# A gated three-branch decoder layer: order of the paired projections, start plan, queue of the merge stores and spacing of the convolution inputs

## The chip, the cores and the metric

The kernel runs on one core of a Trainium2 chip. A core has five engines that run side by side, each through its own list of instructions in order: TensorE (PE, matmuls; the profile shows its weight loads apart as PEld), VectorE (DVE), ScalarE (ACT), GpSimd (POOL) and SyncE (SP, which here only issues DMA transfers). They wait for each other through semaphores. Matmuls read SBUF, the core's working memory, and write PSUM, eight banks of 128 x 512 numbers in float32; DVE and ACT take results out of PSUM. The metric is the time of one execution on the device, in microseconds (us).

## The reference

One layer on x of 1024 positions by 1024 channels (D), everything in float32. Cut to what matters:

```python
u = layer_norm(x) * (1 + scale) + shift            # shift, scale, gate from silu(c) @ w_ada
proj = u @ w_in + b_in                             # 1024 x 12288
a_v, a_g, b_b, b_c, b_h, b_g, c_a, c_b, c_g, merge = split(proj)
y_a = (pool(a_v) grouped @ pool_w) * pool_scale * silu(a_g)      # windows 2, 4, 8, 16
y_b = b_b * dwconv3(b_c * b_h) * silu(b_g)
h_c = dwconv31(c_a * sigmoid(c_b))
y_c = silu(layer_norm(h_c)) * silu(c_g)
m = sum_k sigmoid(merge_k) * (y_k @ w_branch[k])
out = layer_norm(ALPHA * x + gate * (m @ w_out))
```

## The kernel before

**Number form.** Every float32 operand of a matmul is split into a high part (written by ACT, rounded to the fast matmul type) and a low part (DVE: the operand minus its high part). One product of two operands is three matmuls, low x high, high x low and high x high, into one PSUM bank (`mm3`, line 132 is the matmul).

**Channels lie on the partitions**, 128 at a time; one tile is 128 channels by 1024 positions, in two halves of 512. u is transposed at the start, scaled and shifted per channel, and split.

**The work is a list of jobs.** A `Job` is one block of 128 output channels: 16 blocks of input, 48 matmuls. Only the first four jobs (c_a and c_b of two channel blocks) and those of the merges are of this kind. All other projections are 46 `Pair`s: two blocks of 128 output columns at once, as a 2 x 2 block product with seven half-size products in place of eight (84 matmuls of 512 columns). For that, sums and differences of the blocks of u (T1 to T4, made once) and of the weights (S1 to S4, for each pair) are formed on DVE. The seven products, in the order of the program, with their banks and weight tiles:

| product | bank | weights | then |
|---|---|---|---|
| A11 x B11 | px | wa | ACT copies px to the left half of r1 (line 520) |
| A12 x B21 | py | wa | DVE adds py to it (523) |
| S1 x T1 | pz | wb | ACT copies pz to r2 (525) |
| S2 x T2 | px, on top | wb | ACT copies px to the right half of r1 (529) |
| S3 x T3 | px, on top | wc | DVE adds px to r2 (531) |
| S4 x B22 | pz, on top | wc | DVE adds pz to r1 (533) |
| A22 x T4 | px, on top | wd | the pair's `after` takes px as the left half of r2 |

wa, wb and wc of a pair take the three buffers of one pool in turn; so the wb of the next pair takes the buffer of this pair's wb, once S2 has read it. wd has one buffer. Six PSUM banks are there for two pairs.

**What sets the order.** The program issues everything in one order, and the Tile framework's scheduler then moves instructions on each engine by a timeline model of its own. Up to the first pair it doesn't: there the table `START` lists every step by hand, in the order in which it is issued (`p031` is one partial product of job 0, input tile 3, half 1; `T2a`, `T2h0`, `T2l0` the sums for T of channel pair 2, `wah`, `S12` steps of the first pair's weights, and so on). A dependence that only orders, and waits for nothing, is put in by `after(late, early)` with the help of `marks`.

**The convolution of 31 taps** runs on DVE, one instruction of 128 x 1024 for each tap (line 605), eight channel blocks, 240 taps. `conv_step` issues six taps after each job, if an input is there. The inputs come from pairs named c2 to c7, put into the list of jobs at every sixth place. A finished block is stored to DRAM and added to a sum over all channels for the LayerNorm; the first block is copied to a tile of its own for that, `hsum` (615).

**The merges.** After the pairs come 24 jobs z (y_k times w_branch[k], 48 matmuls each, gated by DVE), with the four small pool jobs between the first four. Their inputs (y, the pooled values, the gates, the conv's results) were stored to DRAM by earlier stages and are loaded again by POOL's queue (lines 653, 729, 763, 800, 801, 822); stores go by POOL too (538), and weights by SP's queue (381). A queue issues strictly in order: an entry that waits holds all behind it. Nearly all large tiles share one pool of 37 slots of 128 x 1024.

Of the kernel before, what the change touches and what calls it, by code (L numbers as in the profile page):

```python
# [9 lines left out]
F32 = mybir.dt.float32  # L10
# [6 lines left out]
P = 128  # L17
# [10 lines left out]


ADA_PE = (2, 0, 0, 0)  # L30
LN_ACT = (4, 5, 6, 7)
LOADS = "x0 x1 x2 x3 a0 w0 x4 x5 x6 x7 w1 a2 w2 a4 a6 w3"
START = (
# [12 lines left out]
)  # L46

BIG_SLOTS = 37
# [10 lines left out]
def kernel(  # L59
# [23 lines left out]
    wspl = ctx.enter_context(tc.tile_pool(name="wspl", bufs=W8_BUFS))  # L83
    wsum = ctx.enter_context(tc.tile_pool(name="wsum", bufs=2))
    wlast = ctx.enter_context(tc.tile_pool(name="wlast", bufs=1))
    small = ctx.enter_context(tc.tile_pool(name="small", bufs=4))
    ps_main = ctx.enter_context(tc.tile_pool(name="ps_main", bufs=6, space=PSUM))
    ps_misc = ctx.enter_context(tc.tile_pool(name="ps_misc", bufs=2, space=PSUM))
# [41 lines left out]
    def mm3(ps, wh, wl, rh, rl, start, stop):  # L130
        for n, (w, r) in enumerate(((wl, rh), (wh, rl), (wh, rh))):
            nc.tensor.matmul(  # L132
                ps, w, r, start=start and n == 0, stop=stop and n == 2, skip_group_check=True
            )


    ident = const.tile([P, P], F32, name="ident")
    make_identity(nc, ident)
# [15 lines left out]
    def columns(name, parts, q, cols=None):  # L154

        n = sum(a.shape[0] for a in parts)
        rows = slot(f"{name}_rows")[:n, :P]
        at = 0
        for a in parts:
            q.dma_start(out=rows[at : at + a.shape[0], :], in_=a)  # L160
            at += a.shape[0]
        if cols is None:
            cols = const.tile([P, n], F32, name=name)
        ps = misc_ps(f"{name}_ps")
        nc.tensor.transpose(ps[:, :n], rows, ident[:n, :n])
        nc.scalar.copy(cols, ps[:, :n])
        return cols
# [278 lines left out]
    class Pair:  # L446
# [26 lines left out]
        def step(self, what):  # L473

            raw1, raw2 = self.raw
            a1, a2 = (r.rearrange("p (i q c) -> p q i c", q=2, c=P) for r in self.raw)
            if what[0] == "S":
                t = wsum.tile([P, 2, HALF], F32, tag="sum", name=f"s{what[1:]}_{self.name}")
                self.sums[what[1]] = t.rearrange("p n c -> p (n c)")
                one, two = (t[:, n].rearrange("p (i c) -> p i c", c=P) for n in range(2))  # L480
                if what == "S12":
                    nc.vector.tensor_add(one, a2[:, 0], a2[:, 1])
                    nc.vector.tensor_sub(two, one, a1[:, 0])
                    self.s2 = two
                else:
                    nc.vector.tensor_sub(one, a1[:, 0], a2[:, 0])
                    nc.vector.tensor_sub(two, a1[:, 1], self.s2)
                return
            which, high = what[1], what[2] == "h"
            if high and which == "d":  # L490
                self.w[which] = wlast.tile([P, 2, HALF], F32R, tag="last", name=f"wd_{self.name}")
            elif high:
                self.w[which] = wspl.tile([P, 2, D], F32R, tag="w", name=f"w{which}_{self.name}")
            hi, lo = (self.w[which][:, n] for n in range(2))
            if which == "d":
                src = a2[:, 1]
                hi, lo = (t.rearrange("p (i c) -> p i c", c=P) for t in (hi, lo))
            else:
                src = raw1 if which == "a" else self.sums["1" if which == "b" else "3"]
            if high:  # L500
                nc.scalar.activation(hi, src, AF.Identity)
            else:
                marks["split"] = nc.vector.tensor_tensor(
                    out=lo, in0=src, in1=f32(hi), op=ALU.subtract
                )

        def product(self, ps, left, right, first):
            which, block = self.left[left]
            w = self.w[which]
            for i in range(4):  # L510
                ks = slice(block(i) * P, (block(i) + 1) * P)
                rh, rl = quarter(right, i)
                mm3(ps, w[:, 0, ks], w[:, 1, ks], rh, rl, first and i == 0, i == 3)

        def run(self):
            col1, col2 = self.cols
# [77 lines left out]
    def conv_step(n):  # L594
        while n > 0 and conv_todo:
            item = conv_todo[0]
            j, g, h, s = item
            w = cfw_cols[:, (K31 - 1 - s) * NT + j : (K31 - 1 - s) * NT + j + 1]
            if s == 0:
                h = item[2] = slot(f"h{j}")  # L600
                ins = nc.scalar.activation(h, g, AF.Identity, bias=vec("cf_b", j), scale=w)  # L601
                if j == 0:
                    after(ins, marks["u"])
            else:
                nc.vector.scalar_tensor_tensor(  # L605
                    out=h[:, s:], in0=g[:, : S - s], scalar=w, in1=h[:, s:],
                    op0=ALU.mult, op1=ALU.add,
                )
                n -= 1
            item[3] = s + 1  # L610
            if s == K31 - 1:
                conv_todo.popleft()
                if conv["sum"] is None:
                    conv["sum"] = slot("hsum")
                    nc.scalar.copy(conv["sum"], h)
                else:
                    nc.vector.tensor_add(conv["sum"], conv["sum"], h)
                store(h_dram[j], h)
                conv["n"] += 1
# [35 lines left out]
    def a_pool(g):  # L655
        def run(w):
            for o in range(2):
                ct = 2 * g + o
                ps = [bank(f"pool_ps{ct}_{h}") for h in range(2)]
                for i in range(2):  # L660
                    for h in range(2):
                        ph, pl = pooled[2 * g + i]
                        ws = slice((2 * i + o) * P, (2 * i + o + 1) * P)
                        mm3(
                            ps[h], w[:, 0, ws], w[:, 1, ws], ph[:, HALVES[h]], pl[:, HALVES[h]],
                            i == 0, i == 1,
                        )
                t = sg_a.pop(ct)
                for h in range(2):
                    nc.vector.scalar_tensor_tensor(  # L670
                        out=t[:, HALVES[h]], in0=ps[h], scalar=vec("pool_scale", ct),
                        in1=t[:, HALVES[h]], op0=ALU.mult, op1=ALU.mult,
                    )
                store(y_dram[0][ct], t)

        jobs.append(Job(f"pool{g}", pool_w[0][g], None, None, run=run))

# [87 lines left out]
    def c_square(j):  # L765
        t = c_state.pop(("h", j))
        nc.vector.tensor_sub(t, t, c_state["mean"])
        store(c_dram[j], t)
        sq = slot(f"sq{j}")
        nc.scalar.activation(sq, t, AF.Square)  # L770
        if j == 0:
            c_state["q"] = sq
        else:
            nc.vector.tensor_add(c_state["q"], c_state["q"], sq)
# [28 lines left out]
    def c_y(ct):  # L803
# [3 lines left out]
            n, n, AF.Silu, bias=vec("cf_ln_b", ct), scale=vec("cf_ln_g", ct)  # L807
        )
        nc.vector.tensor_mul(n, n, sg)
        store(y_dram[2][ct], n)  # L810


    y, m, m_hi, m_lo, g_in = {}, {}, {}, {}, {}
# [38 lines left out]
    for b in (1, 0, 2):  # L852
        for i in range(NT // 2):
            light.append(
                lambda b=b, i=i: gates(
                    f"m{b}_{i}", C_M + b * D + 2 * i * P, AF.Sigmoid, g_dram[b][2 * i : 2 * i + 2],
                    nc.sync if (b, i) == (2, NT // 2 - 1) else None,
                )
            )
    heavy = [f for group in todo for f in group]  # L860
# [5 lines left out]
            order.append(light[li])  # L866
            li += 1
    order += light[li:]
    every = 6
    j = CLASSIC // 2  # L870
    for n, f in enumerate(order):
        if n % every == every - 1 and j < NT:
# [94 lines left out]
    for i, job in enumerate(jobs):  # L967
# [10 lines left out]
            f(*args)  # L978
        if 8 <= i < 8 + NT:
            gate_row(i - 8)  # L980
        if n_proj <= i < n_proj + 8 and (i - n_proj) % 2 == 0:
            a_load((i - n_proj) // 2)
        if i == n_a - 2:
            marks["y0"] = marks["split"]
            for k in range(NT):
# [91 lines left out]
```

## Time and profile before

| | |
|---|---|
| median of three runs | 1389.99 us (1388.82 to 1390.48) |
| the profiled execution, as timed | 1390.33 us |
| its span on the core | 1388.6 us |
| PE weight loads (PEld) | 1093.3 us busy, 79% |
| moved by DMA | 188.40 MB, mean 136 GB/s |
| end of the chain that ended last | PE 26%, issue 8%, DMA 2% of the span |

A row of the timeline reads: start, duration, engine, line, operation, output<-inputs, shape, count, and in brackets how long the engine stood idle before and what released it. In a row of waits stand the waiting engine and line, what it waited for, the total, the times and the longest. Matmuls are pipelined: one of 512 columns shows 0.39 us, but the next starts about 0.23 us after it.

### The profile page before, as it was taken

To read this page: it belongs to the slowest core of one execution; us is meant where nothing else is said; L and a number is where in the kernel's file an instruction comes from. 1 tells how busy PE (TensorE), PEld (TensorE's weight loads), DVE (VectorE), ACT (ScalarE), POOL (GpSimd) and SP (SyncE) were. 2 spreads that over 40 slices of the span, in tenths; PEclk is the share of its full clock that TensorE was granted. 3 is DMA by queue.
4 is the path that set the end of the run, shared out by engine and by line. 5 is a ranking of instruction groups with operands and counts; after the bars stand their busy time and mean duration, and the time that the engine had idled before them with its cause. 6 is when DMAs were issued, how large, how long until landed. Compare 5 with 4: busy or idle time off the path is not lost. (4 is left out here: it accounts for less than half of the span.)

```text
span 1388.6 us, 15235 instructions
## 1 busy us (share of the span) xinstructions
PE 1329.0 (96%) x5893; PEld 1093.3 (79%) x5893; DVE 1100.0 (79%) x1292; ACT 528.0 (38%) x652; POOL 113.7 (8%) x220
## 2 busy tenths in 40 slices
PE   4899889999999999999999999999897999999997
PEld 2678678887888888888888888888685888888886
DVE  6999989999999679958985998699645757635576
ACT  4554245343443444535443544444422333312100
POOL 2000000000000000000000000000212232200010
PEclk8999999999999999999999999999998999999999
DMA  9611314442222312322342234324867979712332
GB/s 291 184 46 46 106 48 120 121 137 78 90 92 91 106 44 95 106 76 60 105 152 84 87 106 142 102 76 144 309 215 277 352 271 336 276 61 76 122 107 91
DMA packets 167949, 188.40 MB, mean 136 GB/s; under 512 B 6292, under 2 KB 138820, under 8 KB 167876
## 3 DMA queue, kind: packets, MB, share of 16 engines
q1 hardware_dynamic: 141936, 94.91, 23.1%
q0 software_dynamic: 25408, 92.29, 17.8%
q8 instruction: 46, 0.75, 0.2%
q10 hardware_dynamic: 532, 0.22, 0.1%
q14 instruction: 27, 0.22, 0.0%
HBM read 137.06 MB, written 50.34 MB: 135 GB/s over the span
## 5 line engine op out<-in xcount | busy, mean ns | idle before, releaser
L605 DVE SCALAR_TENSOR_TENSOR h<-r_c,cfw_cols,h 128x1023 f32<-128x1023 f32 (+9 forms) x180 | 227.5, 1264 | 5.6 <-ACT h L601 5.3
L605 DVE SCALAR_TENSOR_TENSOR h<-cs,cfw_cols,h 128x1023 f32<-128x1023 f32 (+29 forms) x60 | 76.0, 1267 | 1.3 <-ACT h L601 1.0
L403 ACT ACTIVATE w_z<-raw_z 128x1024 fp32r<-128x1024 f32 x24 | 25.2, 1060 | 122.0 <-PE ps_z L132 61.0
L827 DVE TENSOR_TENSOR g<-ps_z,g 128x512 f32<-128x512 f32 x48 | 31.7, 688 | 50.2 <-PE ps_z L132 49.7
L132 PE MATMUL ps_p<-u,w_p 128*128 128x512 f32 x192 | 50.6, 414 | 2.5 <-DVE u L341 1.4
L132 PEld LDWEIGHTS ps_p<-u,w_p 128*128 128x128 f32 x192 | 36.4, 197 | 12.8 <-DVE u L341 4.5
L409 DVE TENSOR_TENSOR w_z<-raw_z,w_z 128x1024 fp32r<-128x1024 f32 x24 | 29.1, 1221 | 15.3 <-ACT w_z L403 15.3
L538 POOL DMA_DIRECT2D g_dram<-r_m x22 | 11.7, 533 | 349.3 <-ACT r_m L713 238.0
L132 PE MATMUL py_m<-u,wa_m 128*128 128x512 f32 x144 | 36.2, 389 | 0.0
L132 PE MATMUL ps_z<-y_3h,w_z 128*128 128x512 f32 x96 | 34.0, 391 | 1.1 <-ACT y_3h L127 1.1
L132 PE MATMUL px_m<-u,wa_m 128*128 128x512 f32 x144 | 34.8, 389 | 0.0
L132 PE MATMUL ps_z<-y_0h,w_z 128*128 128x512 f32 x96 | 34.7, 395 | 0.0
L132 PE MATMUL pz_m<-u,wc_m 128*128 128x512 f32 x144 | 34.6, 389 | 0.0
L132 PE MATMUL ps_z<-y_2h,w_z 128*128 128x512 f32 x96 | 33.9, 391 | 0.1
L132 PE MATMUL ps_z<-y_1h,w_z 128*128 128x512 f32 x96 | 33.9, 389 | 0.0
L132 PE MATMUL ps_z<-y_4h,w_z 128*128 128x512 f32 x96 | 33.5, 389 | 0.0
L132 PE MATMUL ps_z<-y_7h,w_z 128*128 128x512 f32 x96 | 33.3, 389 | 0.0
L132 PE MATMUL ps_z<-y_6h,w_z 128*128 128x512 f32 x96 | 33.3, 389 | 0.0
L132 PE MATMUL ps_z<-y_5h,w_z 128*128 128x512 f32 x96 | 33.3, 389 | 0.0
L1027 DVE TENSOR_TENSOR og<-out_ps,gate_b 128x512 f32<-128x512 f32 (+1 forms) x18 | 11.1, 624 | 26.6 <-PE out_ps L132 13.4
L132 PE MATMUL px_m<-t_1h,wb_m 128*128 128x512 f32 x96 | 32.1, 389 | 0.0
L132 PE MATMUL px_m<-t_0h,wc_m 128*128 128x512 f32 x96 | 31.5, 389 | 0.0
(568 smaller groups left out, 3876.7 us busy)
## 6 DMA issues: line engine op xcount, KB each, us to landing
raw_m<-in_w_in_dram SPq DMA_DIRECT2D x24, 512.0 KB
raw_z<-in_w_branch_dram SPq DMA_DIRECT2D x24, 512.0 KB
g<-g_dram POOLq DMA_DIRECT2D x24, 512.0 KB, 8.2
g_dram<-r_m POOLq DMA_DIRECT2D x22, 512.0 KB, 3.7
ada<-in_w_ada_dram SPq DMA_DIRECT2D x32, 256.0 KB
raw_b<-in_w_in_dram SPq DMA_DIRECT2D x16, 512.0 KB
raw_d<-in_w_in_dram SPq DMA_DIRECT2D x16, 512.0 KB
raw_a<-in_w_in_dram SPq DMA_DIRECT2D x16, 512.0 KB
```

The source lines that it names most:

```text
L132: nc.tensor.matmul(ps, w, r, start=start and n == 0, stop=stop and n == 2, skip_group_check=True)
L403: nc.scalar.activation(self.w[:, 0, : self.width], raw, AF.Identity)
L409: marks["split"] = nc.vector.tensor_tensor(out=lo, in0=raw, in1=f32(hi), op=ALU.subtract)
L538: return (q or nc.gpsimd).dma_start(out=dst, in_=src)
L605: nc.vector.scalar_tensor_tensor(out=h[:, s:], in0=g[:, : S - s], scalar=w, in1=h[:, s:], op0=ALU.mult, op1=ALU.add,)
L827: nc.vector.tensor_mul(g[:, HALVES[h]], ps[h], g[:, HALVES[h]])
L1027: nc.vector.tensor_mul(t, ps[q], final["gate"][:, sl])
```

## The change

Five things are changed.

1. *Pairs.* The first matmul of each product of a pair is put behind the last matmul of the product ahead of it in the program (`chained`), and so for the high parts of wa, wb and wc on ACT. The scheduler can no longer mix the products of two pairs.
2. *Start.* `START` is a new table, and `LN_ACT`, the tiles of x that ACT normalises in place of DVE, gains tiles 1 and 3. The rows of small constants get buffers of their own, or those of the weight sums.
3. *Stores.* The stores of y_a, of the centred conv results and of y_c go by SP's queue in place of POOL's, 24 in all, and so do the gates of one more pair (two stores).
4. *Convolution inputs.* The pairs c2 to c7 stand at every fifth place in place of every sixth. `hsum` is gone: the first block itself takes the sum.
5. *Pool loads.* `a_load` is called one job earlier.

```diff
-LN_ACT = (4, 5, 6, 7)
+LN_ACT = (1, 3, 4, 5, 6, 7)
...
-    "l0 l1 r0 n0 r1 l2 l3 r2 n1 r3 n2 n3 t60 t50 a02 e60 a04 a03 t00 a06 e50 a05 sh0 t40 a07 e00 "
+    "l0 l1 r0 n0 r1 l2 b1 l3 r2 n1 n2 r3 b3 n3 a02 t10 a03 a04 t00 e10 a06 sh0 t50 a05 e00 l4 "
...
+    rows_pool = ctx.enter_context(tc.tile_pool(name="rows", bufs=3))
...
+    def chained(ps, wh, wl, rh, rl, first, start, stop):
+
+        for n, (w, r) in enumerate(((wl, rh), (wh, rl), (wh, rh))):
+            ins = nc.tensor.matmul(
+                ps, w, r, start=start and n == 0, stop=stop and n == 2, skip_group_check=True
+            )
+            if n == 0 and first and "product" in marks:
+                after(ins, marks["product"])
+        if stop:
+            marks["product"] = ins
...
-        rows = slot(f"{name}_rows")[:n, :P]
+        if name in ("ada_cols", "bin_cols"):
+            rows = wsum.tile([P, 2, HALF], F32, tag="sum", name=f"{name}_rows")[:n, 0, :P]
+        else:
+            rows = rows_pool.tile([P, P], F32, tag="rows", name=f"{name}_rows")[:n]
...
-                nc.scalar.activation(hi, src, AF.Identity)
+                ins = nc.scalar.activation(hi, src, AF.Identity)
+                if "high" in marks and which != "d":
+                    after(ins, marks["high"])
+                if which != "d":
+                    marks["high"] = ins
...
-                mm3(ps, w[:, 0, ks], w[:, 1, ks], rh, rl, first and i == 0, i == 3)
+                chained(ps, w[:, 0, ks], w[:, 1, ks], rh, rl, i == 0, first and i == 0, i == 3)
...
-                    conv["sum"] = slot("hsum")
-                    nc.scalar.copy(conv["sum"], h)
+                    conv["sum"] = h
...
-                store(y_dram[0][ct], t)
+                store(y_dram[0][ct], t, nc.sync)
...
-        store(c_dram[j], t)
+        store(c_dram[j], t, nc.sync)
...
-        store(y_dram[2][ct], n)
+        store(y_dram[2][ct], n, nc.sync)
...
-                    nc.sync if (b, i) == (2, NT // 2 - 1) else None,
+                    nc.sync if b == 2 and i >= NT // 2 - 2 else None,
...
-    every = 6
+    every = 5
...
-        if n_proj <= i < n_proj + 8 and (i - n_proj) % 2 == 0:
-            a_load((i - n_proj) // 2)
+        if n_proj - 1 <= i < n_proj + 7 and (i - n_proj) % 2 == 1:
+            a_load((i - n_proj + 1) // 2)
```

The order of the instructions, at three places. First PE in pair b3, at the end of S2, before the change (px, py, pz are the banks, u and t the inputs, wb_b3 the weights of S1 and S2, wc_b3 those of S3 and S4; cg3 is the next pair):

```order
L132 MATMUL px_b3_2294<-t3_1h_779,wb_b3_2151 128x512
L132 MATMUL pz_b3_2295<-u1_1_528,wc_b3_2157 128x512 x3
L132 MATMUL pz_b3_2295<-u3_1_592,wc_b3_2157 128x512 x3
L132 MATMUL pz_b3_2295<-u5_1_676,wc_b3_2157 128x512 x3
L132 MATMUL pz_b3_2295<-u7_1_743,wc_b3_2157 128x512 x3
L132 MATMUL px_cg3_2425<-u0_0_487,wa_cg3_2276 128x512 x3
L132 MATMUL px_cg3_2425<-u2_0_692,wa_cg3_2276 128x512 x3
L132 MATMUL px_cg3_2425<-u4_0_687,wa_cg3_2276 128x512 x3
L132 MATMUL px_cg3_2425<-u6_0_728,wa_cg3_2276 128x512 x3
L132 MATMUL py_cg3_2442<-u1_0_497,wa_cg3_2276 128x512 x3
L132 MATMUL px_b3_2294<-t0_0h_937,wc_b3_2157 128x512
```

The same place after the change:

```order
L141 MATMUL px_b3_2428<-t3_1h_820,wb_b3_2287 128x512
L141 MATMUL px_b3_2428<-t3_1l_821,wb_b3_2287 128x512
L141 MATMUL px_b3_2428<-t3_1h_820,wb_b3_2287 128x512
L141 MATMUL px_b3_2428<-t0_0h_909,wc_b3_2293 128x512
L141 MATMUL px_b3_2428<-t0_0l_910,wc_b3_2293 128x512
L141 MATMUL px_b3_2428<-t0_0h_909,wc_b3_2293 128x512
```

Before, 27 matmuls into other banks stand between the last of S2 (with wb) and the first of S3 (with wc); after it, none, and this holds for all 46 pairs. S4 and A22 follow behind S3.

Second ACT at the same place, after the change (line 545 copies pz, 549 copies px after S2, 517 makes high parts):

```order
L540 ACTIVATE r1_b3_2430<-px_b3_2428,bin_cols_131 128x512
L517 ACTIVATE wa_cg3_2410<-raw_cg3_0_2277 128x1024
L545 ACTIVATE r2_b3_2431<-pz_b3_2429,bin_cols_131 128x512
L517 ACTIVATE wb_cg3_2416<-s12_cg3_2413 128x1024
L549 ACTIVATE r1_b3_2430<-px_b3_2428,bin_cols_131 128x512
L517 ACTIVATE wc_cg3_2422<-s34_cg3_2419 128x1024
```

The high part of the next pair's wb stands ahead of the copy of px, in 44 of the 46 pairs; before the change these two stood in the same order.

Third POOL's queue around the load of pool6, before the change (y0_dram are the stores of y_a, hc the conv results, sga the gates of the pool branch):

```order
L538 DMA y0_dram4_166<-sga4_7257 128x1024
L538 DMA y0_dram5_167<-sga5_7259 128x1024
L763 DMA hc0_7372<-h_dram0_154 128x1024
L763 DMA hc1_7374<-h_dram1_155 128x1024
L729 DMA pool6l_7377<-pool_dram6_192 128x1024
L538 DMA c_dram0_234<-hc0_7372 128x1024
```

And after it:

```order
L672 DMA sga4_7203<-sga_dram4_201 128x1024
L672 DMA sga5_7205<-sga_dram5_202 128x1024
L841 DMA g1_2_7212<-g1_dram2_223 128x1024
L748 DMA pool6l_7310<-pool_dram6_195 128x1024
L748 DMA pool7l_7315<-pool_dram7_196 128x1024
L672 DMA sga6_7319<-sga_dram6_203 128x1024
L672 DMA sga7_7321<-sga_dram7_204 128x1024
L841 DMA g1_3_7328<-g1_dram3_224 128x1024
L782 DMA hc0_7391<-h_dram0_157 128x1024
```

The stores of y0 are gone from the queue, and the loads of pool6 and pool7 stand ahead of those of hc.

More of the change, by code (lines that the diff above doesn't have):

```diff
@@ L30 @@
 ADA_PE = (2, 0, 0, 0)
-LN_ACT = (4, 5, 6, 7)
+LN_ACT = (1, 3, 4, 5, 6, 7)
 LOADS = "x0 x1 x2 x3 a0 w0 x4 x5 x6 x7 w1 a2 w2 a4 a6 w3"
 START = (
[12 rows of a table removed]
[12 rows of a table added]
+    "wch wcl "
 )
```

22 rows, old and new, of the table START are left out of this document.

## The prediction

> **What bounds the kernel now.** I read the page's busy table first, then one table by stage, then the waits of TensorE. All times below are on the profiled execution: a span of 1388.6 us, 1390.33 us as timed, so 1.7 us lie outside the span; the median of the three runs shown, 1389.99 us, is 0.3 us below it.
>
> ```profile
> span 1388.6 us, 15235 instructions
> PE 1329.0 (96%) x5893; PEld 1093.3 (79%) x5893; DVE 1100.0 (79%) x1292; ACT 528.0 (38%) x652; POOL 113.7 (8%) x220
> ```
>
> TensorE (PE) is busy for 96% of the span, and no other engine for more than 79%. The stage table says where the other 4% are. Its columns are the stage, then busy us and instructions of PE, PEld, VectorE (DVE), ScalarE (ACT) and POOL, then the granted clock, the DMA share and GB/s.
>
> ```profile
> 0.00:65.00 65.00, 40.78 (x187) 30.62 (x187) 52.23 (x103) 35.21 (x54) 8.91 (x33) 0.89 0.83 254
> 65.00:160.00 95.00, 93.67 (x410) 76.67 (x411) 91.96 (x109) 40.73 (x49) 1.25 (x2) 1.00 0.19 59
> 160.00:185.00 25.00, 15.96 (x62) 12.44 (x61) 21.38 (x21) 8.39 (x11) 1.07 (x2) 0.86 0.21 73
> 185.00:975.00 790.00, 790.00 (x3482) 652.65 (x3481) 686.53 (x759) 344.01 (x439) 31.95 (x60) 1.00 0.32 99
> 975.00:1075.00 100.00, 85.06 (x358) 67.28 (x357) 53.44 (x59) 32.38 (x37) 22.12 (x42) 0.95 0.78 273
> 1075.00:1378.00 303.00, 303.00 (x1398) 253.29 (x1397) 189.37 (x235) 67.23 (x66) 47.45 (x81) 1.00 0.55 193
> 1378.00:1389.00 11.00, 0.51 (x5) 0.30 (x3) 5.12 (x12) 0.00 (x0) 0.92 (x1) 0.72 0.13 48
> ```
>
> From 185 to 975 us, where nearly all the pairs run, PE never pauses: 3482 matmuls in 790 us are 0.2269 us each. That is the price of a matmul wherever nothing is waited for. Time is lost only in the first 65 us (24 us idle), around 160 to 185, and where the merges begin (975 to 1075). With 0.2269 us for each of their matmuls the two later stages lose 25 - 62 x 0.2269 = **10.9 us** and 100 - 358 x 0.2269 = **18.8 us**. The waits of PE give the reasons:
>
> ```profile
> PE pool_ps L132 <- ACT pool6h L127: 10.1, 1, 10.1
> ...
> PE px_b L132 <- ACT r_b L520: 5.9, 1, 5.9
> ...
> PE pz_d L132 <- DVE wb_d L503: 3.1, 1, 3.1
> ```
>
> So the change can win at most these pieces, some 30 us and a part of the start. Whatever stops PE inside the 790 us costs its full length.
>
> **Part 1, kept order of pairs.** In the order before, the fourth product of a pair (S2, into bank px) and the fifth (S3, into px again) never follow each other: the sixth product and pieces of the next pair stand between. Afterwards S3 follows S2 directly in all 46 pairs. S3 may not write px until ACT has copied it to r1 (line 529 before). What that copy takes, the trace shows in every pair, since ACT does it today too:
>
> ```profile
> 105.57 0.39 PE L132 MATMUL px_b<-t_1h,wb_b 128*128 128x512 f32 x1
> ...
> 106.06 1.06 ACT L501 ACTIVATE wb_d<-s_d 128x1024 fp32r<-128x1024 f32 x1 [1.86 <-PE px_b L132]
> 107.02 0.67 ACT L529 ACTIVATE r_b<-px_b,bin_cols 128x512 f32<-128x512 f32 x1
> ...
> 140.93 0.39 PE L132 MATMUL px_cg<-t_1h,wb_cg 128*128 128x512 f32 x1
> 141.16 0.39 PE L132 MATMUL px_d<-t_1h,wd_d 128*128 128x512 f32 x1
> 141.42 1.06 ACT L501 ACTIVATE wb_b<-s_b 128x1024 fp32r<-128x1024 f32 x1 [1.92 <-PE px_cg L132]
> 142.38 0.67 ACT L529 ACTIVATE r_cg<-px_cg,bin_cols 128x512 f32<-128x512 f32 x1
> ...
> 937.64 0.39 PE L132 MATMUL px_m<-t_1h,wb_m 128*128 128x512 f32 x1
> 938.06 1.06 ACT L501 ACTIVATE wb_m<-s_m 128x1024 fp32r<-128x1024 f32 x1 [1.51 <-PE px_m L132]
> 939.03 0.67 ACT L529 ACTIVATE r_m<-px_m,bin_cols 128x512 f32<-128x512 f32 x1
> ```
>
> The last matmul of S2 starts at 140.93. ACT waits for its end, because the next pair's wb takes the buffer that S2 has just read. It does that conversion first (141.42, 1.06 us), and only then the copy, over at 142.38 + 0.67 = 143.05. That is 2.12 us after the last start of S2; read the same way it is 2.06 to 2.49 us in 45 of the 46 pairs (median 2.11). Today PE spends them on another product, 0.23 us after S2 (141.16). Afterwards ACT's order is the same, conversion of wb before the copy, in 44 of 46 pairs, and nothing is left on PE to hide it. How PE comes back from a wait:
>
> ```profile
> 168.90 0.50 PE L132 MATMUL pz_d<-t_0h,wb_d 128*128 128x512 f32 x1 [3.10 <-DVE wb_d L503]
> ...
> 169.24 0.39 PE L132 MATMUL pz_d<-t_0l,wb_d 128*128 128x512 f32 x1
> ...
> 176.17 1.04 ACT L615 COPY hsum<-h 128x1024 f32<-128x1024 f32 x1 [9.28 <-DVE h L605]
> ...
> 177.12 0.68 ACT L520 ACTIVATE r_b<-px_b,bin_cols 128x512 f32<-128x512 f32 x1
> ...
> 177.85 0.80 PE L132 MATMUL px_b<-t_1h,wb_b 128*128 128x512 f32 x1 [5.94 <-ACT r_b L520]
> 178.45 0.63 PE L132 MATMUL px_b<-t_1l,wb_b 128*128 128x512 f32 x1
> 178.88 1.05 PE L132 MATMUL px_b<-t_1h,wb_b 128*128 128x512 f32 x2
> ```
>
> From the copy's end (177.80) to PE's start (177.85) are 0.05 us, and the first matmul after a pause holds the second back by 169.24 - 168.90 - 0.23 = 0.11 us. Each pair therefore loses 2.12 + 0.05 - 0.23 + 0.11 = **2.05 us**, and the two pairs without a conversion ahead lose 2.05 - 0.96 = 1.09: 44 x 2.05 + 2 x 1.09 = **+92 us**. Behind the waiting matmul stand the pair's last three products and all later pairs, so nothing overtakes it. The bounds: 1.09 in all pairs (50 us), and 2.49 - 0.07 = 2.42 in all (111 us).
>
> A second new wait is A22 into px, which needs the DVE addition of px after S3. S4 lies between, 12 x 0.2269 = 2.7 us, against 0.5 us to the addition's start, at most one conv tap ahead of it (1.26) and 0.69 for itself. That is hidden, as long as DVE isn't behind. Its load:
>
> ```profile
> L605 DVE SCALAR_TENSOR_TENSOR h<-r_c,cfw_cols,h 128x1023 f32<-128x1023 f32 (+9 forms) x180 | 227.5, 1264 | 5.6 <-ACT h L601 5.3
> ```
>
> **Part 2, convolution inputs five jobs apart.** The 240 taps are the same. They now fall into the first 40 or so pairs. Outside them a pair costs DVE about (686.5 + 92 - 240 x 1.26) / 46 = 10.4 us, and 240 taps over 40 pairs add 7.6: 18.0 us on average, against a pair period of 84 x 0.2269 + 2.05 = 21.1. On average DVE keeps up, only because PE has become slower. But the order puts up to ten taps into one pair, 10.4 + 10 x 1.26 = 23 us, so DVE can fall behind for a while. I take **+5 us**, from 0 to 20.
>
> **Part 3, first pairs.** The copy of hsum is gone, for which ACT stood 9.28 us (176.17) and PE 5.94. The order that made wb_d late is new too. I take the whole **-10.9 us**; the other end is 0.
>
> **Part 4, merges.** The chain of waits shows what held pool6 for 10.1 us:
>
> ```profile
> 1048.83 0.75 DVE sga L670
> 1049.58 0.28 issue
> 1049.87 0.44 POOL y_dram L538
> 1050.30 0.09 issue
> 1050.39 0.43 POOL hc L763
> 1050.83 0.09 issue
> 1050.92 0.53 POOL hc L763
> 1051.45 9.84 DMA pool6l<-pool_dram
> 1061.30 1.06 ACT pool6h L127
> ```
>
> A store of y0 waited on POOL for DVE, and the load of pool6 stood behind it and behind two loads of hc. Afterwards these stores are in SP's queue, and the pool loads are issued a job earlier and ahead of hc. Likewise the store of the last conv channel no longer stands among the loads of y1, since the conv ends some six pairs sooner. On SP the stores now stand before loads of raw_z, which have four buffers and are needed a job (10.9 us) later. I take **-16 us** of the 18.8; the ends are -18.8 and +5, should a weight wait behind a store.
>
> [...]
>
> **Part 5, the start.** Two of the eight LayerNorm scalings go from DVE to ACT, and more partial products stand before the last input tile, so PE has less left when it arrives; against that the sums T0 and T1 come late, just before the first pair needs them. I take **-2.5 us**; for lack of rows, a third of the 24 us idle either way (-8 to +6). The other pools and the saved tile add no instruction.
>
> **Sum:** 1388.6 + 92.4 + 5 - 10.9 - 16 - 2.5 = 1456.6, with the 1.7 outside **1458 us**.
>
> **Rivals.** (a) *ACT copies first.* If the copy didn't wait for the conversion, the pairs would cost 46 x 1.09 = 50 us: 1416. The printed order and 45 rows speak against it. Chance 0.10. (b) *DVE becomes the bound*: if each A22 waits for one more tap, 46 x 1.26 = 58 us come on top: 1511 without the 5. It decides once DVE is over 1.2 us behind at S3's end. Chance 0.07. (c) *The clock drops in each gap.* After the 5.94 us pause matmuls came 0.43 us apart for some 3.5 us, so about 1.8 us were lost; after 3.10 us there was no such thing. Were it so after 2 us, 46 x 1.8 = 83 us more: 1541. Chance 0.04. [...] (d) *Faster: S3's wait is covered.* If another engine's release let S3 start with S2's end, or the order weren't kept on the chip, the stores and the start would be left: 1388.6 - 29.4 + 1.7 = 1361. It decides where under 0.6 us per pair are exposed. Against it stands that PE runs in its order and S3's bank is the one being read. Chance 0.05.
>
> **How the numbers follow.** Forecast 0.74, rivals as above. The forecast's own range, by the bounds of the parts, is 1440 to 1490. For 8 in 10 it reaches down to (a) and leaves out the rest: **1412 to 1492**. A measurement of this kernel can tell about 0.2% from no change. Faster 0.05, the same 0.01, slower 0.94.
>
> **What would show it.** In the changed profile PE should wait some 46 times, about 1.9 us each, for ACT's copy r1 from px (line 549), 85 to 95 us in total; the stage of the pairs should have no PE share of 100%, at a clock of 1.00. The wait for pool6h should be gone, the waits for r_b and wb_d too. Few waits for the addition at line 551 mean DVE keeps up; many mean (b). A copy ahead of wb's conversion means (a). A PE without these waits would make the prediction wrong altogether.

## The result and the profile after

The changed kernel takes **1472.46 us** (median of 4 runs, 1471.11 to 1473.62) against 1389.4 us before (median of 4): a ratio of 1.06, with a 95% interval of 1.0587 to 1.0613. That is 83 us slower. The forecast was 1458 us, its range 1412 to 1492.

The page's busy table of the changed kernel, two rows:

```profile
span 1471.8 us, 15315 instructions
PE 1362.0 (93%) x5893; PEld 1107.4 (75%) x5893; DVE 1107.0 (75%) x1292; ACT 531.4 (36%) x651; POOL 99.4 (7%) x194
```

The instructions of PE are the same 5893, but it is busy for 33 us more than before (1362.0 against 1329.0). So besides standing still it must have run slower in places. The stage table, with the columns of the one before:

```profile
0.00:65.00 65.00, 45.48 (x209) 36.84 (x210) 53.42 (x109) 39.69 (x58) 8.56 (x33) 0.92 0.82 254
65.00:160.00 95.00, 90.03 (x390) 72.60 (x391) 93.02 (x107) 41.09 (x48) 1.78 (x3) 1.00 0.22 67
160.00:185.00 25.00, 23.22 (x96) 18.68 (x95) 24.60 (x26) 9.31 (x11) 0.00 (x0) 0.93 0.15 42
185.00:975.00 790.00, 724.72 (x3059) 584.08 (x3058) 642.78 (x693) 302.53 (x379) 27.14 (x51) 0.97 0.28 87
975.00:1075.00 100.00, 92.21 (x395) 74.58 (x394) 50.46 (x61) 40.80 (x57) 7.97 (x15) 0.98 0.39 133
```

The stage from 185 to 975 us, where PE was busy for all 790 us before, now has 65 us without a matmul and a granted clock of 0.97 in place of 1.00. 423 fewer matmuls fit into it (3059 against 3482). The waits of PE say for what:

```profile
PE px_m L141 <- ACT r_m L549: 20.1, 12, 1.8
PE px_a L141 <- ACT r_a L549: 14.1, 8, 1.8
PE px_d L141 <- ACT r_d L549: 14.0, 8, 1.8
PE px_b L141 <- ACT r_b L549: 13.2, 8, 1.8
PE px_c L141 <- ACT r_c L549: 10.6, 6, 1.8
PE px_cg L141 <- ACT r_cg L549: 7.1, 4, 1.8
```

These are all 46 pairs, and each waits for the copy at line 549: 79.1 us together. The waits for pool6h (10.1 us), r_b (5.9) and wb_d (3.1) are gone from the list, and no wait for the addition at line 551 has come into it. Two pairs in the timeline, the first at 598 us and the second at 575 us, show the pause and what may follow it:

```profile
598.04 0.39 PE L141 MATMUL px_b<-t_1h,wb_b 128*128 128x512 f32 x1
598.52 1.06 ACT L517 ACTIVATE wb_d<-s_d 128x1024 fp32r<-128x1024 f32 x1 [0.96 <-PE px_b L141]
599.49 0.67 ACT L549 ACTIVATE r_b<-px_b,bin_cols 128x512 f32<-128x512 f32 x1
600.21 0.50 PE L141 MATMUL px_b<-t_0h,wc_b 128*128 128x512 f32 x1 [1.78 <-ACT r_b L549]
...
603.08 1.75 PE L141 MATMUL pz_b<-u,wc_b 128*128 128x512 f32 x7
```

```profile
575.30 0.39 PE L141 MATMUL px_c<-t_1h,wb_c 128*128 128x512 f32 x1
575.78 1.06 ACT L517 ACTIVATE wb_b<-s_b 128x1024 fp32r<-128x1024 f32 x1 [2.09 <-PE px_c L141]
576.75 0.67 ACT L549 ACTIVATE r_c<-px_c,bin_cols 128x512 f32<-128x512 f32 x1
...
577.47 0.50 PE L141 MATMUL px_c<-t_0h,wc_c 128*128 128x512 f32 x1 [1.78 <-ACT r_c L549]
...
578.73 1.05 PE L141 MATMUL px_c<-t_0h,wc_c 128*128 128x512 f32 x2
...
580.01 1.05 PE L141 MATMUL px_c<-t_0h,wc_c 128*128 128x512 f32 x2
...
581.72 1.51 PE L141 MATMUL pz_c<-u,wc_c 128*128 128x512 f32 x5
```

The pause is the same: 598.04 to 600.21 and 575.30 to 577.47 are 2.17 us between the last start of S2 and the first of S3, so 2.17 - 0.23 = 1.94 us are lost. But S3 takes 603.08 - 600.21 = 2.87 us in the first pair and 581.72 - 577.47 = 4.25 in the second, where from 578.7 on the matmuls come 0.43 us apart. I call the latter a *drop* of the clock, and count one where S3 takes over 3.7 us. The granted clock that the trace records agrees: 3.41 us at 0.5 stand behind each pause so counted, and behind no other. Read so, the 46 pairs of this profile have 86.4 us of pauses, 14 drops of 1.56 us beyond 12 x 0.2269, and 0.15 us at each restart of the other 32 (4.7 us): **113.0 us** in all.

The starts of the first and the last matmul of the pairs divide the span in three. Those of the versions in which a part was tried alone (below) stand with them:

| kernel | to the first pair, us | pairs, us | behind them, us | span, us |
|---|---|---|---|---|
| before | 94.9 | 891.7 | 402.0 | 1388.6 |
| changed | 88.5 | 995.7 | 387.5 | 1471.8 |
| changed, order of products free | 90.6 | 882.1 | 384.4 | 1357.0 |
| before, only hsum's copy gone | 93.6 | 880.6 | 400.3 | 1374.4 |
| before, only stores and pool loads | 94.8 | 892.0 | 385.8 | 1372.6 |
| before, only the start | 89.8 | 894.4 | 401.0 | 1385.2 |

The change loses 104 us in the pairs, and wins 6.4 ahead of them and 14.5 behind them.

### The profile page after: what moved, and what is told of

The parts are those of the page before. It is cut to its first block, busy times and chain, and to the rows that moved or that the text cites. A ratio compares the mean times of both kernels' runs of the same rounds, so it can differ in the third digit from the quotient of the medians.

```text
span 1471.8 us, 15315 instructions
## 1 busy us (share of the span) xinstructions
PE 1362.0 (93%) x5893; PEld 1107.4 (75%) x5893; DVE 1107.0 (75%) x1292; ACT 531.4 (36%) x651; POOL 99.4 (7%) x194
## 3 DMA queue, kind: packets, MB, share of 16 engines
q0 software_dynamic: 21664, 78.66, 14.8%
## 5 line engine op out<-in xcount | busy, mean ns | idle before, releaser
L425 DVE TENSOR_TENSOR w_z<-raw_z,w_z 128x1024 fp32r<-128x1024 f32 x24 | 29.2, 1221 | 29.9 <-ACT w_z L419 29.9
L134 PE MATMUL ps_p<-u,w_p 128*128 128x512 f32 x192 | 49.9, 414 | 0.3 <-DVE u L357 0.2
L141 PEld LDWEIGHTS px_m<-t_0h,wc_m 128*128 128x128 f32 x96 | 18.6, 194 | 28.9 <-ACT r_m L549 25.1
L141 PE MATMUL px_a<-t_0h,wc_a 128*128 128x512 f32 x64 | 27.2, 492 | 14.1 <-ACT r_a L549 14.1
L141 PE MATMUL px_b<-t_0h,wc_b 128*128 128x512 f32 x64 | 24.2, 441 | 13.2 <-ACT r_b L549 13.2
L141 PE MATMUL px_d<-t_0h,wc_d 128*128 128x512 f32 x64 | 23.3, 427 | 14.0 <-ACT r_d L549 14.0
L523 DVE TENSOR_TENSOR wb_m<-s_m,wb_m 128x1024 fp32r<-128x1024 f32 x12 | 14.7, 1222 | 25.3 <-ACT wb_m L517 25.3
```

The costliest lines, as they stand in the source:

```text
L134: nc.tensor.matmul(ps, w, r, start=start and n == 0, stop=stop and n == 2, skip_group_check=True)
L141: ins = nc.tensor.matmul(ps, w, r, start=start and n == 0, stop=stop and n == 2, skip_group_check=True)
L425: marks["split"] = nc.vector.tensor_tensor(out=lo, in0=raw, in1=f32(hi), op=ALU.subtract)
L523: marks["split"] = nc.vector.tensor_tensor(out=lo, in0=src, in1=f32(hi), op=ALU.subtract)
```

## The experiments

All ratios are to the kernel before, run on the same chip in the same session.

### What the kept order costs

The first version is the changed kernel without the kept order of the products; all other parts stay, the order of the high parts on ACT too.

```diff
-                chained(ps, w[:, 0, ks], w[:, 1, ks], rh, rl, i == 0, first and i == 0, i == 3)
+                mm3(ps, w[:, 0, ks], w[:, 1, ks], rh, rl, first and i == 0, i == 3)
```

> The changed kernel, with the order of the seven products left to the scheduler again; everything else of the change stays. Theory (the kept order alone costs the 46 pauses of 1.9 us and the slow clock behind them, 117 us in the stage of the pairs): 1472 - 117 = 1355 us, and no wait for line 549 above 0.2 us. Rival A (DVE becomes the bound once PE is fast again, since up to ten taps fall into one pair): 1365 to 1385 us, with waits of PE for DVE between 100 and 900 us. Rival B (the loss sits in other parts of the change: start, stores, the order of the high parts on ACT): above 1440 us.

Measured: **1357.52 us**, ratio 0.977 (0.9754 to 0.9787), the fastest version of this study. In its profile the stage of the pairs is full again:

```profile
185.00:975.00 790.00, 790.00 (x3482) 652.61 (x3481) 691.90 (x763) 347.88 (x444) 40.92 (x77) 1.00 0.34 108
```

So the kept order of the products costs 1472.5 - 1357.5 = 115 us, of which the 113.0 us read above are the pauses and drops. DVE, at 691.90 of 790 us, doesn't hold PE.

The opposite test adds only the kept order (and that of the high parts on ACT) to the kernel before; `chained` is the function of the change.

```diff
-                mm3(ps, w[:, 0, ks], w[:, 1, ks], rh, rl, first and i == 0, i == 3)
+                chained(ps, w[:, 0, ks], w[:, 1, ks], rh, rl, i == 0, first and i == 0, i == 3)
```

> The kernel before, with only the kept order of products and of ACT's high parts added; start, convolution inputs and stores stay as before. Theory (this part alone costs 46 x 1.88 = 87 us of pauses, 46 x 0.15 = 7 us of slow restarts and 1.5 us behind one pause in three, 23 us): 1389 + 117 = 1506 us, a few us less where the old waits of the first pairs fall into the pauses. Rival (the pauses come from the new start or the denser convolution): below 1440 us.

Measured: 1500.16 us, ratio 1.0794 (1.0766 to 1.0822). The waits of PE in its profile:

```profile
PE px_m L139 <- ACT r_m L544: 20.1, 12, 1.8
PE px_b L139 <- ACT r_b L544: 14.2, 8, 1.8
...
PE px_b L139 <- ACT r_b L535: 9.0, 1, 9.0
PE pool_ps L132 <- ACT pool6h L127: 8.2, 1, 8.2
```

The pauses are those of the changed kernel (87.4 us, 15 drops), and the old waits for r_b and pool6h are still there. So the new start and the denser convolution aren't needed for the pauses.

### Is it the keeping, or who stands next to whom?

The order stays kept, but in `Pair.run` S2 is put ahead of S1. Then A12 lies between A11 and S2, S1 between S2 and S3, and S4 between S3 and A22: no two products into px are neighbours.

```diff
+            self.product(px, "S2", "T2", False)
+            nc.scalar.activation(r1[:, RIGHT], px, AF.Identity, bias=bias(col1))
             self.product(pz, "S1", "T1", True)
...
-            self.product(px, "S2", "T2", False)
-            nc.scalar.activation(r1[:, RIGHT], px, AF.Identity, bias=bias(col1))
             self.product(px, "S3", "T3", False)
```

> The changed kernel, its order of products still kept, but S2 now ahead of S1, so that S1 (12 matmuls, 2.72 us) lies between S2 and S3. Theory (not the keeping but the neighbourhood of S2 and S3 costs: the copy ends 1.9 us after S2, and 2.72 us of matmuls now cover it): about 1355 us, PE without waits in the pairs, clock 1.00 there. Rival A (DVE falls behind and A22 waits for its addition at line 551): 1365 to 1400 us with PE waits on DVE. Rival B (a kept order costs by itself, since PE can no longer go round a late weight): above 1400 us with waits for wb or wc at line 523.

Measured: 1370.03 us, ratio 0.9861 (0.9847 to 0.9876). Two lines exchanged take back 102 of the 115 us. The rest fits rival A, with a second wait beside it:

```profile
PE px_d L141 <- DVE r_d L551: 2.4, 2, 1.8
PE px_m L141 <- DVE r_m L551: 2.3, 1, 2.3
PE px_m L141 <- ACT r_m L540: 2.1, 1, 2.1
...
PE px_c L141 <- DVE r_c L551: 1.6, 2, 1.0
```

With 0.2 us at r_b these are 8.6 us of the 9.4 by which the two spans differ (1366.4 and 1357.0). I took them for too many taps per pair, and gave DVE more room: `every = 6` in that version.

```diff
-    every = 5
+    every = 6
```

> The kernel with S2 ahead of S1, with the convolution inputs six jobs apart again instead of five. Theory (its 12 us above the version with a free order are waits for DVE's addition, since DVE has too many taps per pair): at six apart DVE has more room, the 6.5 us of waits for line 551 fall below 3 us, and the time is 1364 us. Rival (the taps keep DVE late at six apart as well, since conv_step hands out up to ten taps a pair either way): 1370 us with the same waits.

Measured: 1377.72 us, ratio 0.9918 (0.9904 to 0.9933), so slower still. The theory fell: the waits for line 551 went from 6.5 to 4.5 us only, and one wait of 5.7 us came for the copy r_m at line 540, with two stretches of 3.41 us at half the clock along with it (929.99 to 936.82). The timeline of ACT shows what held that copy (the sums s of a pool pair, made on DVE at line 653, have their heads copied by ACT at line 652):

```profile
927.88 0.19 ACT L652 COPY s<-s 128x4 f32<-128x4 f32 x1 [0.33 <-DVE s L653]
928.85 1.27 DVE L625 SCALAR_TENSOR_TENSOR h<-r_c,cfw_cols,h 128x1006 f32<-128x1006 f32 x1
...
930.02 1.22 DVE L653 TENSOR_TENSOR s<-s 128x1020 f32<-128x1020 f32 x1
...
931.32 0.20 ACT L652 COPY s<-s 128x8 f32<-128x8 f32 x1 [3.25 <-DVE s L653]
931.43 0.68 ACT L540 ACTIVATE r_m<-px_m,bin_cols 128x512 f32<-128x512 f32 x1
```

ACT stood 3.25 us at a copy of 0.2 us, which waited for DVE's sum behind a conv tap, and the copy that PE needed stood behind it. At six apart the conv still has taps in the pool pairs (its last one ends at 956 us, against 842 us at five apart). The kernel before, six apart with the order free, has no such wait in its list; which rearrangement avoids it was not tried.

The other neighbour: S4 instead of S1 between S2 and S3, so that A22 follows S3 directly.

```diff
+            self.product(pz, "S4", "B22", False)
+            nc.vector.tensor_add(r1[:, RIGHT], pz, r1[:, RIGHT])
             self.product(px, "S3", "T3", False)
             nc.vector.tensor_add(r2[:, RIGHT], px, r2[:, RIGHT])
-            self.product(pz, "S4", "B22", False)
-            nc.vector.tensor_add(r1[:, RIGHT], pz, r1[:, RIGHT])
```

> The changed kernel, order of products kept, with S4 put between S2 and S3; A22 then comes right behind S3. Theory (a kept order only moves the pause to the next neighbours on px: A22 waits for DVE's addition, some 0.5 us to its start, 0.69 for itself, and half a conv tap ahead of it in the first 40 pairs): 46 pauses of about 1.4 us at line 553's or 551's addition, and a few drops of the clock: 1357 + 64 + 7 = 1428 us, with bounds 1410 and 1450. Rival (the addition is early enough): 1357 us.

Measured: 1457.9 us, above the bounds. The pause moved to A22, as expected, but it is often longer than I took it for. Not only taps stand ahead of the addition on DVE, but also parts of weights, sums of the pool branch and, as here, a product of line 718:

```profile
282.19 1.22 DVE L718 TENSOR_TENSOR r_d<-r_d,r_b 128x1024 f32<-128x1024 f32 x1
283.32 0.68 DVE L553 TENSOR_TENSOR r_d<-px_d,r_d 128x512 f32<-128x512 f32 x1
...
284.06 0.78 PE L141 MATMUL px_d<-t_1h,wd_d 128*128 128x512 f32 x1 [3.57 <-DVE r_d L553]
```

The waits for line 553 sum to 69.7 us, up to 3.6 us each; from the starts of the matmuls the 46 pauses are 80 us, against the 64 expected, and 12 drops come on top. Both kept orders with neighbours in one bank paid for them, here at A22 and in the changed kernel at S3.

### The pause itself: ACT's order and the clock

Here the adjacent S2 and S3 stay, but the next pair's wb, and the steps behind it (S34, wc, wd), are prepared behind the copy of px instead of ahead of it. The part of the edit that hands over the next pair is left out here.

```diff
             nc.scalar.activation(r1[:, RIGHT], px, AF.Identity, bias=bias(col1))
+            late = marks.pop("late", None)
+            if late is not None:
+                late.prepare(("wbh", "wbl", "S34", "wch", "wcl", "wdh", "wdl"))
             self.product(px, "S3", "T3", False)
```

> The changed kernel with its adjacent S2 and S3, but the preparation of the next pair's wb is issued behind the copy of px, so that ACT makes the copy first. Theory (1.06 us of each pause is ACT's conversion; the pause without it is the 0.94 us that the first and the last pair show, and pauses that short drop no clock): 1355 + 46 x 0.94 + 46 x 0.15 = 1405 us, and S3 takes 2.9 us in all pairs. Rival A (the clock drops behind short pauses too, in one of three): 1405 + 14 x 1.5 = 1426 us. Rival B (wb comes too late now and PE waits for it at S1 instead): above 1440 us.

Measured: **1407.3 us**, ratio 1.0131 (1.0116 to 1.0147). The pause is 0.93 or 0.94 us in all 46 pairs (43.0 us), S3 takes 2.85 to 2.90 us in each, and there is no drop:

```profile
566.57 0.39 PE L141 MATMUL px_b<-t_1h,wb_b 128*128 128x512 f32 x1
566.99 0.69 ACT L549 ACTIVATE r_b<-px_b,bin_cols 128x512 f32<-128x512 f32 x1 [0.90 <-PE px_b L141]
567.58 1.05 ACT L517 ACTIVATE wb_d<-s_d 128x1024 fp32r<-128x1024 f32 x1
567.73 0.50 PE L141 MATMUL px_b<-t_0h,wc_b 128*128 128x512 f32 x1 [0.78 <-ACT r_b L549]
```

So ACT's conversion was 86.4 - 43.0 = 43 us of the pauses, and no pause of 0.94 us brought a drop. The next version makes the copy of px twice (line 549 repeated) in the changed kernel, to lengthen the pause.

```diff
             nc.scalar.activation(r1[:, RIGHT], px, AF.Identity, bias=bias(col1))
+            nc.scalar.activation(r1[:, RIGHT], px, AF.Identity, bias=bias(col1))
             self.product(px, "S3", "T3", False)
```

> The changed kernel with ACT's copy of px made twice, so that each pause grows from 1.94 to about 2.6 us. Theory (the clock is set by stretches of 3.4125 us, and drops where a pause of 1.9 us or more lies within one; so longer pauses meet the condition more often): 46 x 0.67 = 31 us for the pauses, and about 32 drops instead of 14, 1.45 us each, 26 us: 1472 + 57 = 1529 us. Rival (drops come at random in one pause of three, whatever its length): 1472 + 31 = 1503 us with 14 drops. Rival (each pause above 2 us drops the clock): 46 drops, 1550 us.

Measured: 1535.48 us, ratio 1.1052 (1.1018 to 1.1085). The pauses are 2.60 us, 118.2 in all, with 34 drops (32 expected). The 3.4125 us of the expectation stand in the trace of the changed kernel as 3.413. The same repetition was added to the version with the copy first.

```diff
             nc.scalar.activation(r1[:, RIGHT], px, AF.Identity, bias=bias(col1))
+            nc.scalar.activation(r1[:, RIGHT], px, AF.Identity, bias=bias(col1))
             late = marks.pop("late", None)
```

> The kernel of the run with ACT's copy first, and this copy made twice: pauses of about 1.6 us instead of 0.94. Theory (pauses below about 1.9 us drop no clock): 1407 + 46 x 0.67 = 1438 us and no drop, S3 at 2.9 us everywhere. Rival (drops in proportion to the pause): 46 x 1.6 / 1.94 / 3.3 = some 11 drops, 1454 us.

Measured: 1520.98 us. The edit missed its aim: ACT ran the conversion between the two copies, and the pause became 2.46 us instead of 1.6. So a version with pauses of 1.6 us throughout is missing, and the expectation of no drop was not put to the test. But this gives one more length, with 28 drops among the 44 pauses of 2.46 us. The five profiles together, each line worked out from the starts of PE's matmuls in the timeline as above:

| kernel | pauses, us | drops among pauses of its usual length | all losses, us | 1357.5 + losses | measured |
|---|---|---|---|---|---|
| copy first | 43.0 | 0 of 46 (0.94 us) | 49.9 | 1407.4 | 1407.3 |
| changed | 86.4 | 14 of 31 (1.94 us), 0 of 13 (1.88) | 113.0 | 1470.5 | 1472.5 |
| before, kept order only | 87.4 | 15 of 32 (1.94 us), 0 of 13 (1.88) | 115.4 | 1504.5 (on 1389.1) | 1500.2 |
| copy first, twice | 111.8 | 28 of 44 (2.46 us) | 161.0 | 1518.5 | 1521.0 |
| copy twice | 118.2 | 34 of 44 (2.60 us) | 175.7 | 1533.2 | 1535.5 |

Pauses, restarts and drops account for each version to within 4.3 us, and for those on 1357.5 to within 2.5.

### The parts that win

Each was put alone into the kernel before. First the convolution inputs five apart, without the copy of hsum:

```diff
-                    conv["sum"] = slot("hsum")
-                    nc.scalar.copy(conv["sum"], h)
+                    conv["sum"] = h
...
-    every = 6
+    every = 5
```

> The kernel before with only the convolution inputs five jobs apart and the copy of hsum gone. Theory (this is what removes the waits of 9.0 us and the 2.4 us at a lower clock between 160 and 185 us): 1389 - 11 = 1378 us, and no wait for r_b or wb_d there. Rival A (the denser taps make DVE late with PE at full speed): 1385 to 1400 us. Rival B (those waits belong to the start's order): 1389 us.

Measured: 1377.49 us, ratio 0.9915 (0.99 to 0.993). Both waits are gone. Then only the copy of hsum is gone, and the inputs stay six apart:

```diff
-                    conv["sum"] = slot("hsum")
-                    nc.scalar.copy(conv["sum"], h)
+                    conv["sum"] = h
```

> The kernel before with only the copy of hsum gone; the convolution inputs stay six jobs apart. Theory (the copy, for which ACT stood 9.28 us, is what held r_b, and the low clock followed from that pause): 1389 - 8 = 1381 us, no wait for r_b near 176 us, the one for wb_d of 3.1 us stays. Rival (the spacing of the convolution inputs removes the waits, and the copy is innocent): 1389 us with both waits.

Measured: 1376.34 us, ratio 0.991 (0.9893 to 0.9926), the same. Both waits are gone here too, and PE is busy from 160 to 185 us at a clock of 1.00:

```profile
160.00:185.00 25.00, 25.00 (x112) 20.72 (x111) 24.58 (x25) 9.53 (x12) 0.53 (x1) 1.00 0.21 65
```

So taking out the copy is enough for the whole gain, and the spacing adds nothing to it that can be measured. That the wait for wb_d would go too was not expected. It can't have been the running copy that made wb_d late, since PE waited until 168.90 and the copy started at 176.17: with the copy out of the program the scheduler puts the instructions in another order, in which ACT makes the high part of wb_d at 161.75 us instead of 165.84. Next the stores and pool loads (the other stores are changed as in the change itself):

```diff
-                store(y_dram[0][ct], t)
+                store(y_dram[0][ct], t, nc.sync)
...
-        if n_proj <= i < n_proj + 8 and (i - n_proj) % 2 == 0:
-            a_load((i - n_proj) // 2)
+        if n_proj - 1 <= i < n_proj + 7 and (i - n_proj) % 2 == 1:
+            a_load((i - n_proj + 1) // 2)
```

> The kernel before with only the stores of y0, c_dram, y2 and one more pair of gates on SP's queue and the loads of the pool branch one job earlier. Theory (the load of pool6 stood behind a store that waited for DVE): the wait of 10.1 us for pool6h goes, with what lies around it 14.5 us: 1375 us. [...]

Measured: 1374.08 us, ratio 0.9887 (0.9871 to 0.9904). The wait for pool6h is gone, and 16 us of the stage behind the pairs (402.0 to 385.8). The stores and the earlier loads were not tried apart. Last the start, with its table, its LayerNorm tiles and its buffers for rows:

```diff
-LN_ACT = (4, 5, 6, 7)
+LN_ACT = (1, 3, 4, 5, 6, 7)
```

> The kernel before with only the new start, its choice of LayerNorm tiles for ACT and the tiles of its own for rows. Theory (the pairs began 6.4 us sooner in the changed kernel, and that is all it brings): 1383 us. Rival (it also removes the late wb_d of the first pairs): 1376 to 1380 us. Rival (it needs the other parts, alone nothing): 1389 us.

Measured: 1387.03 us, ratio 0.9982 (0.9973 to 0.9991), so less than the theory's 6 us. The pairs begin 5.1 us sooner, and 2.7 of these are lost again in the pairs, where the waits around 170 us are still there:

```profile
PE px_b L134 <- ACT r_b L525: 5.7, 1, 5.7
...
PE pz_d L134 <- DVE wb_d L508: 2.4, 1, 2.4
```

Copy, stores and start together are -12.5 - 14.8 - 1.9 = -29.2 us, each from the medians of its session; all parts but the kept order of the products won 1389.1 - 1357.5 = 31.6.

## Why the prediction was right, and where it was off

- **Part 1, the pauses.** Forecast +92.4 us for pauses and restarts. Measured 86.4 + 46 x 0.15 = 93.3. The place (S3 for the copy at line 549), the count (46), ACT's order and the price per pair (2.05 us forecast; 1.94 + 0.15 measured in most pairs) were right. The sum of waits was announced as 85 to 95 us and is listed as 79.1, since the list counts from the modelled end of the last matmul.
- **The clock: the step that was off.** The prediction gave the drops no term in the sum and a rival of all or nothing ("Were it so after 2 us, 46 x 1.8 = 83 us more", chance 0.04), from two pauses of the old trace, one with a drop and one without. It announced "a clock of 1.00". What came is a share: 14 of 46 pairs, 14 x (1.56 - 0.15) = 20 us, at 0.97. The mechanism of the rival was right and its count wrong. Two pauses with opposite outcomes don't give a threshold of length: where a pause falls decides too, as the last section shows.
- **Part 2, DVE late: +5 forecast, 0 found.** No wait for line 551 in the changed kernel. That DVE had room because PE was slow, as the prediction argued, fits the version with S2 ahead of S1: there PE is fast, the order kept, and the same waits do appear (6.5 us). It wasn't tested by itself.
- **Part 3, first pairs: -10.9 forecast, -12.5 measured** with the copy of hsum alone. The prediction named that copy. The wait for wb_d, put down to the new order, goes with the copy too, by way of the order that the scheduler then chooses; the new start alone leaves 2.4 of its 3.1 us.
- **Part 4, merges: -16 forecast, -14.8 measured.** That fits the chain of waits, in which a store held the load in POOL's queue; the run moved the stores and issued the loads earlier at once, so the share of each is not shown. The conv that ends sooner, named beside it, shows no gain of its own (1377.5 us with it, 1376.3 without).
- **Part 5, the start: -2.5 forecast, -1.9 measured** alone.
- **The sum.** Forecast +68 us to the median, measured +83: 20 us of drops that were left out, 5 us for DVE that weren't needed. That the time still lies in the range is luck in part. Had the other 32 pauses brought drops as well, 32 x 1.41 = 45 us more, it would have been outside, and against that the prediction had only the one pause of 3.10 us without a drop. The narrower range of 1440 to 1490 doesn't follow from the bounds of the parts either: added end to end they give 1403 to 1532.
- **The rivals.** (a) didn't happen, but where it was brought about its price held: 50 us forecast, 49.9 measured. (b) and (d) didn't happen; the free order shows what (d) would have been (1361 forecast, 1357.5 measured).

## What to carry to other kernels

Before an order is fixed by hand, look for neighbours that use one bank, and take the price of each from the old trace: the time from the producer's last start to the end of the copy, less what still stands between them. Fixing an order can also take away the room in which an engine goes round a late partner: an arrangement with the gaps well filled (S2 ahead of S1) still lost 12.5 us to the free one. And a pause of PE must be priced with the clock that may follow it: here 14 of the 46 pauses brought a drop of 1.56 us each.

## What the runs showed of the hardware that was not expected

The drops are neither random nor a matter of length alone. The trace records the granted clock itself as stretches with a start and a length. In the fourteen profiles every change of the clock lies, to within 0.01 us, on a grid of 3.413 us of its profile, though the kernels differ; the granted clock is 1.00 or 0.50. Here are five stretches of that grid in the changed kernel, two around the pair with the drop and three around the pair without (the columns are those of the stage table; the clock stands behind POOL):

```profile
575.31:578.72 3.41, 1.63 (x7) 1.05 (x6) 1.82 (x2) 1.63 (x2) 0.00 (x0) 1.00 0.14 40
578.72:582.13 3.41, 3.41 (x9) 2.65 (x8) 0.96 (x3) 0.00 (x0) 0.00 (x0) 0.50 0.00 0
...
595.78:599.20 3.42, 2.65 (x12) 1.87 (x10) 1.57 (x2) 2.46 (x3) 0.00 (x0) 1.00 0.54 153
599.20:602.61 3.41, 2.40 (x10) 1.99 (x11) 3.41 (x4) 0.96 (x2) 0.00 (x0) 1.00 0.00 0
602.61:606.02 3.41, 3.41 (x16) 2.82 (x15) 3.41 (x5) 0.00 (x0) 0.00 (x0) 1.00 0.00 0
```

The pause from 575.53 to 577.47 lies whole in one stretch, and the next stretch runs at 0.50. The pause from 598.27 to 600.21 is cut by the border at 599.20 into 0.93 and 1.01 us, and the clock stays at 1.00. So it is with the 230 pauses of the five profiles whose losses the experiments compare. Take for each pause the most of it that falls into one stretch: below 1.84 us none of 128 is followed by a stretch at half the clock, from 1.95 us on all 60 are, and between the two 32 of 42; in the changed kernel alone, none of the 32 up to 1.88 us and all 14 from 1.93 us on. So in these profiles the granted clock follows, one stretch later, how long PE stood still within a stretch. The count of drops then depends on the length of the pauses and on where they happen to fall: 14 of 31 and 15 of 32 pauses of 1.94 us, 28 of 44 of 2.46 and 34 of 44 of 2.60, and none of the 49 of 0.94 and the 26 of 1.88.

The same period comes out of the matmuls alone. Take the times at which S3 restarts in pauses over 1.9 us, as remainders of a fixed period: for a period of 3.4135 us, and among those from 2.5 to 8 us in steps of 0.0005 us for no other, the restarts with a drop and those without fall into two separate stretches in each of the four profiles that have drops (153 such pauses).

Idle time in one stretch is not the whole rule. In the kernel before, the pause of 5.94 us took up 2.8 and 3.3 us of two stretches, and each of the two was followed by one at half the clock; but the pause of 3.10 us had 2.1 us in one, and no drop came. Why is open.
